# A two-layer decoder step on one core: the eight sample columns move from the second token half to the first, one memory's keys and values move to another stage, and the closing norm is done by tokens

## The chip, the core and the metric

The kernel runs on one core of a Trainium2 chip. The core has a matrix engine (TensorE, in the profile PE, with PEld for its weight loads), a vector engine (VectorE, DVE), a scalar engine for activations (ScalarE, ACT), GpSimdE (POOL) and a queue that issues most transfers (SyncE, SP). The metric is the device time of one execution in microseconds, lower is better.

## The reference

One inference step of a decoder with two layers, model width 1024, in float32. There are two inputs which share all weights: a prompt of 1024 tokens, and 8 samples of one token each with caches of their own.

- Layer 0 has a gated linear recurrence (4 heads, state 128 x 128 each) in parallel with attention into 256 memory tokens (4 heads). The two outputs are joined and multiplied by `w_o`.
- After layer 0 one shared key and value (4 heads x 128) is projected with `w_kv`. Layer 1 has stick-breaking attention over these in parallel with memory attention.
- Each layer ends with a SwiGLU feed-forward of width 2816. Every sub-layer is `h = h + rmsnorm(f(rmsnorm(h, g_in)), g_out)`.
- For the samples the recurrence starts from a given state, the memory's keys and values are read from `cache_mem_k` and `cache_mem_v` (512 KB each for a sample and a layer), and the shared keys and values from a paged cache through `page_table`.
- Memory keys and values of the prompt are `mem_prompt @ w_mem_kv[l]` for each layer `l`, and are outputs too.

```python
q_h, f_h, i_h, g_h, q_m = jnp.split(hn @ w_in, 5, axis=-1)
...
o, S = hgrn2_scan(q, k, v, logf, s0)
o = rmsnorm(o, hg_gain) * silu(g_h)
om = mem_attend(q_m, mem_k, mem_v)
out = jnp.concatenate([o, om], axis=-1) @ w_o
...
h = h + rmsnorm(mix, g[1])
h = h + rmsnorm(swiglu(rmsnorm(h, g[2]), w_gu[l], w_down[l]), g[3])
```

## The kernel before

The prompt is split into two halves of G = 512 tokens, called g = 0 and g = 1. Activations lie transposed: 128 features on the partitions, tokens along the row, eight such tiles for the width of 1024. In the kernel before, the 8 samples are eight more columns (512 to 519) of the second half. NG gives a half's width (512, 520), and since one PSUM bank holds 512 columns, a projection of the wider half is done as two pieces of 260 (PW, NPC).

A projection (`proj`, L256) works on float32 as two rounded parts, high and low: for each of 128 rows of weights it issues three matmuls (high x high, high x low, low x high; L264). Weights come in tiles of 256 KB (`split_w`, DMA L245 on SP), ACT rounds them to the high part (L250) and DVE subtracts for the low part (L251). Five raw and five split tiles rotate. `mmp` holds two PSUM tiles for projections, `smp` three, `nsp` one (`NS()`) that the norms, the memory's transposes and the transposes in `residual` share.

Tiles come from rotating pools. The ones that matter here: `cpool` (`C()`, four buffers of 512 KB, for cache tiles, memory tokens, output rows), `apool` (`A()`, eight, recurrence tensors and layer 1 queries), `rpool` (one buffer, the feed-forward's sum or the prompt's rows), `xpool` (normed inputs, eight for each half). A tile that is asked for waits until the buffer's last reader is done.

Stages are generators, one for each head, block or group. `weave((gen, n), ...)` steps several in the ratio of their numbers, `drain` runs one to its end. That fixes the order in which work is written; a scheduler then makes one fixed list of instructions for each engine, and each engine works through its list in order, waiting where data or a buffer is missing.

The stages in order (L1060 to L1113): the first half's input (`start`, rows are scaled with their norm, transposed at L350), its recurrence inputs (`fq`, `v`), its recurrence (`core`: at seven levels, products L810 on PE and updates L815 to L820 on DVE) woven with the memory's keys and values of both layers; then the second half's input and projections, first half's memory attention (L550 to L581) and output product `o0.mm`, the second half's recurrence (`core`, with the samples' recurrence `hgrn_sample` first, L764 and L767) woven with the first half's feed-forward (`f0.part(0)` to `part(4)`), and so on, with one half's attention beside the other half's feed-forward.

A sample's memory attention (`mem_attn_sample`) has no matmul against the cache: the query is transposed (L597), written to memory and read back onto all partitions (L601, L607), each cache tile is multiplied by it (L608) and reduced (L609) on DVE; after the softmax, each value tile is multiplied (L620), its halves added (L621) and summed over partitions with a matmul (L622). `sb_sample` does the same with tiles gathered through the page table on POOL (L649). `sample_scores` and `sample_pv` hold these loops. In layer 0 they run beside `f0.part(2)` and `part(3)`, in layer 1 likewise.

The end of the kernel: `f1.finish` takes the sum of squares over features with a matmul by ones (L291), Ln and Exp (L292, L293), then for each of eight tiles scales (L382) and adds the residual stream from memory (L388); `store_y` transposes back to rows of tokens (L1042), copies (L1045) and stores (L1047, the samples L1056).

## Time and profile before

| | before |
|---|---|
| runs, us | 2579.38, 2580.38, 2580.97 (median 2580.38) |
| profiled execution, us | 2580.92, of which the span is 2579.2 |
| mean granted clock of TensorE | 0.986 of full speed |
| PE busy | 2538.2 us, 98% |
| PE weight loads, beside it | 2211.0 us, 86% |
| DVE busy | 1563.1 us, 61% |
| ACT busy | 1209.4 us, 47% |
| POOL busy | 47.7 us, 2% |
| read from and written to HBM | 267.57 and 31.93 MB, 116 GB/s over the span |

The profile shows one execution. Busy time counts an engine's own instructions; matmuls overlap in TensorE's pipeline, so that a busy PE can still be a slow one, and its price for one matmul is better read from the distance of two starts. In a row of the order of time stand the start and the length in microseconds, the engine, line, operation, output and inputs, and in square brackets the idle time ahead of it with what ended it. The granted clock of TensorE is in tenths of full speed.

### The profile page before, as it was taken

Reading aid. Unit: us, or ns where it says so; the run is one execution under the profiler, and the core shown is the slowest. Engines: PE = TensorE matmul, PEld = TensorE weight load, DVE = VectorE, ACT = ScalarE, POOL = GpSimd, SP = SyncE. Lnnn points to the kernel's source line nnn. Section 1 sums busy time; section 2 is a strip of 40 time slices with the busy share of each in tenths; the row PEclk is TensorE's granted clock in tenths of the full one; section 3 lists DMA queues with packets and bytes.
Section 4 is the critical chain, followed back from the end, with each engine's and each line's share of the span. In section 5 each row is a group of like instructions: output and inputs, shape, how many; then the busy total and the mean of one; then the engine's idle time right before and its main releaser. Section 6 shows DMA issues by size and latency. Waiting matters only on the chain.

```text
span 2579.2 us, 40377 instructions
## 1 busy us (share of the span) xinstructions
PE 2538.2 (98%) x15603; PEld 2211.0 (86%) x15603; DVE 1563.1 (61%) x2717; ACT 1209.4 (47%) x2274; POOL 47.7 (2%) x59
## 2 busy tenths in 40 slices
PE   8999999999999999999999999999999999999997
PEld 6888887888877888999999989767776788999997
DVE  6666475635765576555544576666678658444445
ACT  6446551245334455555433455566542355443333
POOL 1000000000000000000000000000041000000000
PEclk9999997899999999999999999999999999999998
DMA  6352244132652445322333445322166444323332
GB/s 183 109 168 74 71 153 121 37 87 86 186 166 83 130 149 183 101 85 61 99 91 93 126 148 184 110 87 67 56 186 204 147 152 131 111 84 108 93 91 87
DMA packets 459435, 302.16 MB, mean 117 GB/s; under 512 B 17765, under 2 KB 422834, under 8 KB 459242
## 3 DMA queue, kind: packets, MB, share of 16 engines
q1 hardware_dynamic: 456682, 291.18, 37.6%
q0 software_dynamic: 2560, 8.39, 1.1%
q8 instruction: 123, 2.02, 0.3%
q14 instruction: 70, 0.57, 0.1%
HBM read 267.57 MB, written 31.93 MB: 116 GB/s over the span
## 4 chain that ended last, share of the span: by engine, by line
PE 45%; DVE 2%; issue 1%; DMA 1%; ACT 1%; POOL 0%; DVEq 0%; POOLq 0%; ACTq 0%; SPq 0%
PE mm L264 40%; PE s L980 1%; PE s L992 1%; PE s L965 1%; POOL c L649 0%; PE s L622 0%; PE s L1042 0%; PE ns L291 0%; PE s L581 0%; DMA b<-qd 0%; DVE c L608 0%; DVE sc L609 0%; PE s L550 0%; DVE ws L251 0%; DVE st L302 0%
## 5 line engine op out<-in xcount | busy, mean ns | idle before, releaser
L264 PE MATMUL mm<-x,ws 128*128 128x260 f32 (+1 forms) x10080 | 1672.7, 323 | 10.6 <-DVE ws L251 4.2
L264 PEld LDWEIGHTS mm<-x,ws 128*128 128x128 f32 x10080 | 1448.1, 189 | 174.6 <-issue 26.8
L251 DVE TENSOR_TENSOR ws<-w,ws 128x512 fp32r<-128x512 f32 (+1 forms) x800 | 522.8, 658 | 524.5 <-ACT ws L250 521.9
L250 ACT CAST ws<-w 128x512 fp32r<-128x512 f32 (+1 forms) x800 | 474.3, 593 | 713.3 <-PE mm L264 652.5
L264 PE MATMUL mm<-m,ws 128*128 128x260 f32 (+1 forms) x3168 | 541.1, 325 | 0.7 <-ACT r L399 0.7
L264 PEld LDWEIGHTS mm<-m,ws 128*128 128x128 f32 x3168 | 454.1, 188 | 60.9 <-issue 15.8
L277 ACT ACTIVATE t<-mm 128x520 f32<-128x520 f32 (+1 forms) x104 | 62.5, 601 | 189.7 <-PE mm L264 189.7
L401 DVE TENSOR_TENSOR r<-r,mm 128x520 f32<-128x520 f32 (+1 forms) x128 | 88.4, 691 | 88.9 <-PE mm L264 87.6
L447 DVE TENSOR_TENSOR t<-t,mm 128x512 f32<-128x512 f32 (+1 forms) x88 | 60.9, 692 | 73.3 <-PE mm L264 73.1
L280 DVE SCALAR_TENSOR_TENSOR t<-mm,t 128x520 f32<-128x520 f32 (+1 forms) x104 | 72.2, 694 | 42.4 <-ACT t L279 42.1
L302 DVE TENSOR_TENSOR st<-st,n 128x512 f32<-128x512 f32 (+1 forms) x98 | 67.2, 693 | 7.3 <-ACT n L301 5.6
L281 ACT ACTIVATE t<-t 128x520 f32<-128x520 f32 (+1 forms) x104 | 65.9, 633 | 10.3 <-DVE t L280 10.2
L279 ACT ACTIVATE t<-t 128x520 f32<-128x520 f32 (+1 forms) x104 | 66.0, 635 | 2.7
L278 ACT ACTIVATE t<-t 128x520 f32<-128x520 f32 (+1 forms) x104 | 66.2, 637 | 0.0
L283 DVE TENSOR_TENSOR t<-t,mm 128x512 f32<-128x512 f32 (+1 forms) x88 | 60.4, 686 | 5.5 <-ACT t L281 5.0
L271 ACT CAST m<-t 128x512 fp32r<-128x512 f32 (+1 forms) x88 | 54.9, 624 | 17.1 <-DVE t L447 10.0
L272 DVE TENSOR_TENSOR m<-t,m 128x512 fp32r<-128x512 f32 (+1 forms) x88 | 61.1, 694 | 2.6 <-ACT m L271 0.4
L810 PEld LDWEIGHTS s<-a,a 128*128 128x128 f32 x448 | 57.6, 206 | 1.6 <-PE s L810 0.7
L810 PE MATMUL s<-a,a 128*128 128x64 f32 x448 | 57.9, 286 | 0.5 <-DVE a L817 0.5
L649 POOL DMA_INDIRECT c<-in_cache_sb_k,pidx x16 | 22.7, 1416 | 1882.9 <-DVE r L401 1256.9
L944 DVE SCALAR_TENSOR_TENSOR b<-b,b 128x512 f32<-128x512 f32 (+3 forms) x48 | 26.8, 558 | 30.6 <-ACT b L943 30.1
L561 ACT ACTIVATE b<-s,nmx 128x256 f32<-128x256 f32 x64 | 29.8, 470 | 28.8 <-DVE nmx L555 28.8
(262 smaller groups left out, 1969.9 us busy)
## 6 DMA issues: line engine op xcount, KB each, us to landing
w<-in_w_gu SPq DMA_DIRECT2D x352, 256.0 KB, 2.9
w<-in_w_down SPq DMA_DIRECT2D x160, 256.0 KB, 2.8
w<-in_w_in_a SPq DMA_DIRECT2D x80, 256.0 KB, 3.0
w<-in_w_o SPq DMA_DIRECT2D x64, 256.0 KB, 2.7
w<-in_w_mem_kv SPq DMA_DIRECT2D x32, 256.0 KB, 3.0
c<-in_cache_mem_k SPq DMA_DIRECT2D x16, 512.0 KB, 4.6
c<-in_cache_mem_v SPq DMA_DIRECT2D x16, 512.0 KB, 3.9
w<-in_w_kv SPq DMA_DIRECT2D x32, 256.0 KB, 2.8
```

The lines of the kernel that those rows point to most:

```text
L250: nc.scalar.copy(ws[:, 0, :n, :], raw[:, :n, :])
L251: nc.vector.tensor_sub(ws[:, 1, :n, :], raw[:, :n, :], ws[:, 0, :n, :].bitcast(F32))
L264: nc.tensor.matmul(ps[:, a, : PW[g]], wt, xt[k][:, xi, o : o + PW[g]], start=(k == 0 and wi == 0), stop=(k == nk - 1 and wi == 2),)
L272: nc.vector.tensor_sub(dst[1], src, dst[0].bitcast(F32))
L277: nc.scalar.activation(av, pv(ps, g), AF.Abs)
L278: nc.scalar.activation(av, av, AF.Exp, scale=-1.0)
L279: nc.scalar.activation(av, av, AF.Ln, bias=1.0)
L280: nc.vector.scalar_tensor_tensor(av, pv(ps, g), 0.0, av, op0=ALU.min, op1=ALU.subtract)
L281: nc.scalar.activation(av, av, AF.Exp)
L302: nc.vector.tensor_add(acc[:, :n], acc[:, :n], t[:, :n])
L401: nc.vector.tensor_add(dst, dst, pv(ps, g))
L810: nc.tensor.matmul(plv[:, hh, c, :], K_[:, hh, cs], rhs, start=True, stop=True)
```

## The change

- The 8 sample columns belong to the first half: NG is (520, 512), and all conditions on `g` that concern samples turn round. The samples are read and normed in `start(0)`; `hgrn_sample` is a stage of its own, `a0.sample()`, beside `a0.gate()` and `start(1)`; layer 0's `mem_sample` stands behind `a0.mem()` beside the second half's `fq` and `v`, ahead of `o0.mm`; layer 1's `sb_sample` and `mem_sample` belong to `b0` and stand beside `f1.part(0)` to `part(3)`.
- The second half's V lies in two `cpool` tiles instead of `apool` tiles.
- `mem_load` is done once for each layer, into one tile of `rpool`; layer 1's memory keys and values, and the second half's memory queries, move from the first recurrence to `o0.finish()`, the first output norm.
- The closing norm is by tokens: the last `out_proj` (`last=True`) does not store the residual stream, `token_rows` transposes it to rows, the last feed-forward (`rows=True`) scales its tiles with the gain and transposes the first half of them as soon as four are ready (`first_half`), and `finish_rows` takes the norm per token (a matmul with one column for each 128 tokens), transposes the other four tiles, scales and adds in one step for each half row, and stores.
- Layer 1's second half: its attention stands beside `f0.part(0)` to `part(2)`, and `o1.finish` beside `part(3)`.

```diff
--- before.py
+++ after.py
@@ -38,9 +38,9 @@
     NP = page_table.shape[1]
     SCALE = P ** -0.5
     G = 512
-    NG = [G, G + NB]
-    PW = [G, (G + NB) // 2]
-    NPC = [1, 2]
+    NG = [G + NB, G]
+    PW = [(G + NB) // 2, G]
+    NPC = [2, 1]
     WID = G + NB
     CH = G // P
 
@@ -232,10 +232,10 @@
 
 
     def pv(ps, g):
-        return ps[:, 0, :G] if g == 0 else ps[:, :, : PW[1]]
+        return ps[:, 0, :G] if g else ps[:, :, : PW[0]]
 
     def sv(ap, g):
-        return ap[:, :G] if g == 0 else ap.rearrange("p (a n) -> p a n", a=2)
+        return ap[:, :G] if g else ap.rearrange("p (a n) -> p a n", a=2)
 
     def split_w(W, k0, nk, m0):
         out = []
@@ -329,12 +329,13 @@
             xtok.append(rpool.tile([P, CH, D], F32, tag="r", name="xtok1"))
             for tb in range(CH):
                 nc.sync.dma_start(xtok[g][:, tb, :], x_prompt[0, g * G + tb * P : g * G + (tb + 1) * P, :])
+        if g == 0:
             xs = C().rearrange("p a n -> p (a n)")[:NB]
             nc.sync.dma_start(xs, x_sample.rearrange("b o d -> (b o) d"))
         for tb in range(CH):
             rms_rows(xtok[g][:, tb, :], P)
             yield
-        if g:
+        if g == 0:
             ps = S()
             for k in range(ND):
                 nc.tensor.transpose(ps[:, k * NB : (k + 1) * NB], xs[:, k * P : (k + 1) * P], ident[:NB, :NB])
...
@@ -405,8 +406,8 @@
     class out_proj:
 
 
-        def __init__(self, g, l, store):
-            self.g, self.l, self.store, self.x = g, l, store, []
+        def __init__(self, g, l, store, last=False):
+            self.g, self.l, self.store, self.x, self.last = g, l, store, [], last
 
         def mm(self, xo, m0=0, m1=ND):
             g = self.g
@@ -422,16 +423,32 @@
             g, l = self.g, self.l
             rstd = rstd_from(self.acc, NG[g], 1.0 / D)
             acc = small([P, WID], tag="st", bufs=3)
-            yield from residual(g, self.R, rstd, lambda k: gcol(l, 1, k), True, acc, l == 0)
+            yield from residual(g, self.R, rstd, lambda k: gcol(l, 1, k), not self.last, acc, l == 0)
             r2 = rstd_from(acc, NG[g], 1.0 / D)
             yield
-            yield from normed(g, self.R, r2, lambda k: gcol(l, 2, k), self.x)
+            yield from normed(g, self.R, r2, lambda k: gcol(l, 2, k), self.x, self.last)
+
+    def token_rows(g, R):
+
+        ht = []
+        for c in range(CH):
+            t = apool.tile([P, D], F32, tag="a", name=nm("hT"))
+            for a in range(2):
+                ps = S()
+                for k in range(4):
+                    nc.tensor.transpose(ps[:, k * P : (k + 1) * P], R[4 * a + k][:, c * P : (c + 1) * P], ident)
+                nc.scalar.copy(t[:, a * 512 : (a + 1) * 512], ps)
+            ht.append(t)
+            yield
+        htok.append(ht)
+
+    htok = []
 
     PARTS = [(0, 5), (5, 5), (10, 4), (14, 4), (18, 4)]
 
     class ffn:
-        def __init__(self, g, l, xt):
-            self.g, self.l, self.xt = g, l, xt
+        def __init__(self, g, l, xt, rows=False):
+            self.g, self.l, self.xt, self.rows = g, l, xt, rows
             self.R = self.acc = None
 
         def part(self, pi):
@@ -456,6 +473,12 @@
             for m in range(ND):
                 ps = proj(g, w_down[l], f0, nf, m * P, mids)
                 evac_raw(g, self.R, ps, m, self.acc, pi == 0, last)
+                if last and self.rows:
+                    nc.scalar.activation(
+                        self.R[m][:, :n], self.R[m][:, :n], AF.Copy, scale=gcol(l, 3, m)
+                    )
+                    if m == 3:
+                        self.first_half()
                 if m % 2:
                     yield
 
@@ -467,11 +490,41 @@
                 self.r = rstd_from(acc, NG[self.g], 1.0 / D)
                 yield
 
-
-    memt = []
-
-    def mem_load():
-        memt.extend(xpool.tile([P, 2, 2, NM], F32R, tag="x1", name=nm("memt")) for _ in range(ND // 2))
+        def first_half(self):
+            self.yt = [xpool.tile([P, D], F32, tag="x0", name=nm("yT")) for _ in range(CH)]
+            for c in range(CH):
+                ps = S()
+                for k in range(4):
+                    nc.tensor.transpose(ps[:, k * P : (k + 1) * P], self.R[k][:, c * P : (c + 1) * P], ident)
+                nc.scalar.copy(self.yt[c][:, :512], ps)
+
+        def finish_rows(self):
+
+            ht = htok[0]
+            g, R, acc = self.g, self.R, self.acc
+            ps = NS()
+            for c in range(CH):
+                nc.tensor.matmul(ps[:, c : c + 1], acc[:, c * P : (c + 1) * P], ones[:, 0:1], start=True, stop=True)
+            r = small([P, 8], tag="rr")
+            nc.scalar.activation(r[:, :CH], ps[:, :CH], AF.Ln, scale=1.0 / D, bias=epsb)
+            nc.scalar.activation(r[:, :CH], r[:, :CH], AF.Exp, scale=-0.5)
+            for c in range(CH):
+                o = c * P
+                pt = S()
+                for k in range(4):
+                    nc.tensor.transpose(pt[:, k * P : (k + 1) * P], R[4 + k][:, o : o + P], ident)
+                yt, h, rc = self.yt[c], ht[c], r[:, c : c + 1]
+                nc.vector.scalar_tensor_tensor(yt[:, :512], yt[:, :512], rc, h[:, :512], op0=ALU.mult, op1=ALU.add)
+                nc.vector.scalar_tensor_tensor(yt[:, 512:], pt, rc, h[:, 512:], op0=ALU.mult, op1=ALU.add)
+                t0 = g * G + c * P
+                nc.sync.dma_start(y_prompt[0, t0 : t0 + P, :], yt)
+                yield
+
+
+    memt = [None, None]
+
+    def mem_load(l):
+        memt[l] = rpool.tile([P, ND, 2, NM], F32R, tag="r", name=nm("memt"))
         for tb in range(NM // P):
             xt = C()
             xf = xt.rearrange("p a n -> p (a n)")
@@ -480,12 +533,8 @@
                 ps = NS()
                 for k in range(4):
                     nc.tensor.transpose(ps[:, k * P : (k + 1) * P], xf[:, (a + k) * P : (a + k + 1) * P], ident)
-                for b in range(2):
-                    d = memt[(a + 2 * b) // 2]
-                    split_to(
-                        (d[:, 0, :, tb * P : (tb + 1) * P], d[:, 1, :, tb * P : (tb + 1) * P]),
-                        ps[:, 2 * b * P : (2 * b + 2) * P].rearrange("p (k t) -> p k t", k=2),
-                    )
+                d = memt[l][:, a : a + 4, :, tb * P : (tb + 1) * P]
+                split_to((d[:, :, 0, :], d[:, :, 1, :]), ps.rearrange("p (k t) -> p k t", k=4))
             yield
 
     def mem_keys(l):
...
@@ -698,13 +747,13 @@
             )
 
     def v_proj(g, W, m0, xt, vt, vs):
-        vt.extend((A(), A()))
+        vt.extend((C(), C()) if g else (A(), A()))
         for h in range(H):
             ps = proj(g, W, 0, ND, m0 + h * P, xt)
             t = T()
             nc.scalar.copy(sv(t, g), pv(ps, g))
             to_token(t, vt, h)
-            if g:
+            if g == 0:
                 nc.vector.tensor_copy(vs[:, h, :], t[:, G : G + NB])
             yield
 
@@ -866,7 +915,7 @@
             self.g, self.xt = g, xt
             self.W = w_in_a[0]
             self.F, self.K, self.Q, self.V, self.Qm, self.sg = [], [], [], [], [], []
-            self.vs = small([P, H, NB], tag="vs", bufs=1) if g else None
+            self.vs = None if g else small([P, H, NB], tag="vs", bufs=1)
 
         def fq(self):
             yield from gate_proj(self.g, self.W, self.xt, self.F, self.K)
@@ -875,10 +924,11 @@
         def v(self):
             yield from v_proj(self.g, self.W, 8 * P, self.xt, self.V, self.vs)
 
+        def sample(self):
+            yield from hgrn_sample(self.F, self.K, self.Q, self.vs)
+
         def core(self):
             g = self.g
-            if g:
-                yield from hgrn_sample(self.F, self.K, self.Q, self.vs)
             yield from hgrn_prompt(g, self.F, self.K, self.Q, self.V)
             if g:
                 nc.sync.dma_start(st_prompt[0, 0].rearrange("h k v -> k h v"), carry)
...
@@ -1061,23 +1111,19 @@
     drain(start(0, x0))
     a0 = mixer_a(0, x0)
     drain(a0.fq(), a0.v())
-    weave(
-        (a0.core(), 22),
-        (chain(mem_load(), mem_keys(0), mem_values(0), mem_keys(1), mem_values(1), a0.qm(M)), 22),
-    )
+    weave((a0.core(), 22), (chain(mem_load(0), mem_keys(0), mem_values(0), a0.qm(M)), 14))
     a0.open()
     a1 = mixer_a(1, x1)
-    weave((chain(a0.gate(), a0.merge()), 8), (start(1, x1), 14))
-    weave((a0.mem(), 8), (a1.fq(), 8))
+    weave((a0.sample(), 6), (a0.gate(), 4), (start(1, x1), 12))
+    weave((chain(a0.merge(), a0.mem(), a0.mem_sample()), 32), (chain(a1.fq(), a1.v()), 12))
     o0 = out_proj(0, 0, M)
     drain(o0.mm(a0.xo))
-    weave((o0.finish(), 17), (a1.v(), 4))
+    weave((o0.finish(), 17), (chain(mem_load(1), mem_keys(1), mem_values(1), a1.qm(A)), 14))
     f0 = ffn(0, 0, o0.x)
-    weave((a1.core(), 27), (f0.part(0), 9), (a1.qm(A), 4))
+    weave((a1.core(), 22), (f0.part(0), 9))
     a1.open()
-    weave((chain(a1.gate(), a1.merge()), 8), (f0.part(1), 9))
-    weave((chain(a1.mem_sample(), a1.mem()), 28), (chain(f0.part(2), f0.part(3)), 16))
-    drain(f0.part(4))
+    weave((chain(a1.gate(), a1.merge(), a1.mem()), 16), (chain(f0.part(1), f0.part(2)), 17))
+    drain(f0.part(3), f0.part(4))
     xk0, xb0 = [], []
     o1 = out_proj(1, 0, M)
     drain(o1.mm(a1.xo, 0, 1))
@@ -1089,8 +1135,11 @@
     weave((b0.heads(), 8), (o1.finish(), 17))
     b0.open()
     f1 = ffn(1, 0, o1.x)
-    weave((chain(b0.sb(), b0.mem()), 24), (chain(f1.part(0), f1.part(1)), 18))
-    drain(f1.part(2), f1.part(3), f1.part(4))
+    weave(
+        (chain(b0.sb(), b0.mem(), b0.sb_sample(), b0.mem_sample()), 64),
+        (chain(f1.part(0), f1.part(1), f1.part(2), f1.part(3)), 34),
+    )
+    drain(f1.part(4))
     xk1, xb1 = [], []
     o0 = out_proj(0, 1, M)
     drain(o0.mm(b0.xo, 0, 1))
@@ -1102,15 +1151,14 @@
     weave((b1.heads(), 8), (o0.finish(), 17))
     b1.open()
     f0 = ffn(0, 1, o0.x)
-    weave((chain(b1.sb(), b1.mem()), 40), (chain(f0.part(0), f0.part(1)), 18))
-    weave((chain(b1.sb_sample(), b1.mem_sample()), 40), (chain(f0.part(2), f0.part(3)), 16))
-    o1 = out_proj(1, 1, A)
+    weave((chain(b1.sb(), b1.mem()), 40), (chain(f0.part(0), f0.part(1), f0.part(2)), 26))
+    o1 = out_proj(1, 1, A, True)
     drain(o1.mm(b1.xo))
-    weave((o1.finish(), 17), (f0.part(4), 8))
-    f1 = ffn(1, 1, o1.x)
-    weave((chain(f0.finish(False), store_y(0, f0.R)), 12), (f1.part(0), 9))
-    drain(f1.part(1), f1.part(2), f1.part(3), f1.part(4))
-    drain(f1.finish(False), store_y(1, f1.R))
+    weave((o1.finish(), 17), (f0.part(3), 8))
+    drain(f0.part(4))
+    f1 = ffn(1, 1, o1.x, True)
+    weave((chain(f0.finish(False), store_y(0, f0.R), token_rows(1, o1.R)), 21), (chain(f1.part(0), f1.part(1)), 18))
+    drain(f1.part(2), f1.part(3), f1.part(4), f1.finish_rows())
 
 
 _INS = [
```

16 lines of the change are left out of this document (8 added, 8 removed).

## The prediction

> **What bounds the kernel now.** I read the head of the page first (busy shares and the clock), then the busy time by stretch, then the order of time at the places where TensorE (PE) falls short. The median of the three runs is 2580.38 us; the profiled execution took 2580.92 us, 0.02% above it, and the sum below is made against 2580.92.
>
> ```profile
> span 2579.2 us, 40377 instructions
> PE 2538.2 (98%) x15603; PEld 2211.0 (86%) x15603; DVE 1563.1 (61%) x2717; ACT 1209.4 (47%) x2274; POOL 47.7 (2%) x59
> PEclk9999997899999999999999999999999999999998
> ```
>
> PE is busy for 98%, DVE for 61%: the span is the length of PE's stream, and a change gains only where PE idles or runs slowly. The granted clock dips around the seventh slice and at the end. By stretch (columns: span, then PE, PEld, DVE, ACT and POOL busy, clock, DMA share, GB/s):
>
> ```profile
> 380.00:400.00 20.00, 20.00 (x105) 14.62 (x104) 15.54 (x22) 5.71 (x10) 0.00 (x0) 0.92 0.57 158
> 400.00:420.00 20.00, 20.00 (x61) 14.22 (x59) 5.19 (x7) 0.62 (x1) 0.00 (x0) 0.50 0.53 144
> 420.00:440.00 20.00, 19.96 (x103) 16.96 (x104) 13.73 (x28) 5.78 (x12) 0.00 (x0) 0.90 0.35 120
> 460.00:480.00 20.00, 19.50 (x138) 19.26 (x137) 18.55 (x65) 0.62 (x1) 0.00 (x0) 0.80 0.10 27
> 480.00:500.00 20.00, 17.80 (x79) 14.96 (x79) 6.06 (x17) 6.75 (x12) 0.00 (x0) 0.78 0.05 14
> 660.00:720.00 60.00, 60.00 (x266) 48.87 (x265) 47.26 (x63) 26.22 (x45) 0.00 (x0) 1.00 0.72 215
> 1900.00:1920.00 20.00, 15.77 (x58) 11.96 (x57) 20.00 (x23) 6.01 (x10) 15.14 (x9) 0.83 0.77 238
> 1980.00:2000.00 20.00, 16.31 (x65) 12.53 (x64) 19.91 (x25) 7.05 (x12) 0.00 (x0) 0.94 0.74 235
> ```
>
> These stretches are, in order: the samples' recurrence (hgrn_sample, at 0.92, 0.50 and 0.90), the end of the second half's recurrence, layer 0's sample memory attention, which costs PE nothing (60.00 of 60), and layer 1's two sample score phases, in which DVE is full (20.00) and PE waits. Prices on PE come from starts that follow each other:
>
> ```profile
> 428.40 5.73 PE L264 MATMUL mm<-x,ws 128*128 128x512 f32 x24
> 433.97 1.90 PE L810 MATMUL s<-a,a 128*128 128x64 f32 x16
> 441.24 5.47 PE L810 MATMUL s<-a,a 128*128 128x64 f32 x48
> 446.79 5.78 PE L264 MATMUL mm<-x,ws 128*128 128x512 f32 x24
> 454.79 5.99 PE L264 MATMUL mm<-x,ws 128*128 128x260 f32 x48
> 460.62 8.46 PE L810 MATMUL s<-a,a 128*128 128x64 f32 x74
> L381 PE MATMUL ns<-ident,ht 128*128 128x128 f32 x64 | 9.8, 275 | 0.0
> ```
>
> A 512-column matmul takes (433.97 - 428.40)/24 = 0.232 us, two of 260 take 2 x (460.62 - 454.79)/48 = 0.243, a 64-column one (446.79 - 441.24)/48 = 0.116. A 128-column transpose lies between 0.116 and 9.8/64 = 0.153; I take 0.12.
>
> **The change part by part.**
>
> *Sample columns to the first half, as such.* The count of projections in the form with 2 x 260 columns equals that with 512 in both programs: 0. What counts is where the sample work lands.
>
> *The tail (closing norm by tokens).*
>
> ```profile
> 2544.83 7.50 PE L264 MATMUL mm<-m,ws 128*128 128x260 f32 x61
> 2553.83 0.70 DVE L302 TENSOR_TENSOR st<-st,n 128x520 f32<-128x520 f32 x1 [0.76 <-ACT n L301]
> 2556.91 0.27 ACT L292 ACTIVATE st<-ns,epsb 128x8 f32<-128x8 f32 x1 [0.48 <-PE ns L291]
> 2557.88 1.43 DVE L382 SCALAR_TENSOR_TENSOR r<-r,par,st 128x520 f32<-128x520 f32 x2 [3.35 <-ACT st L293]
> 2571.09 3.12 SPq L1047 DMA_DIRECT2D out_y_prompt<-c  x4
> 2575.51 0.30 SPq L1056 DMA_DIRECT2D out_y_sample<-c  x1
> ```
>
> Now the last projection ends at 2544.83 + 7.50 = 2552.3, and 26.9 us follow: sum of squares, norm, eight pairs of DVE steps, transposes, copies, stores. Afterwards: the same 2.2 to the sum of squares (2552.3 to 2554.5), eight matmuls of one column at 0.116 with the 0.48 that ACT waited ahead of L292, 1.4, Ln and Exp on four columns 0.6 (two of 0.27 and a handover), eight steps on DVE at 1.43/2 = 0.72, 5.7, and the last store, 4 (the sample store of before ends 3.7 after its issue at 2575.51; this one is 512 KB). Together 14: a gain of 13 (10 to 14). The transposes lie before or beside this.
>
> *More work on PE outside the tail.* 16 transposes of the second mem_load, 32 of token_rows, 16 of first_half, and the samples' 8 of store_y, out of the tail now: 72 x 0.12 = 8.6; I take 8. Nothing covers it, since PE is the bound. The 8 ACT scalings, the ACT copies and the smaller number of splits lie on engines with room: 0; without that cover 16 such steps, at the 0.72 of L382, would be 11.5. The eight stores and four loads of hs less on SP: 0, since PE waits for none of them.
>
> *Layer 1's samples.*
>
> ```profile
> L608 DVE TENSOR_TENSOR c<-c,b 128x1024 f32<-128x1024 f32 x24 | 29.0, 1223 | 5.3 <-DMA b<-qd 5.3
> L609 DVE TENSOR_REDUCE sc<-c 128x8 f32<-128x1024 f32 x24 | 28.9, 1215 | 0.0
> L621 DVE TENSOR_TENSOR c<-c 128x512 f32<-128x512 f32 x24 | 16.0, 687 | 0.0
> ```
>
> They leave the second half (lines sb_sample, mem_sample) and stand beside four parts of the first half's feed-forward instead of two. Lost now: idle 4.2 + 3.7, and by the clock 20 x 0.17 + 20 x 0.06 = 4.6, together 12.5. In the new order one score phase stands beside some 150 projections of 0.232, that is 35 us; DVE has 8 x (1.22 + 1.22) = 19.5 us of scores and, for each 48 matmuls (11 us), some nine steps of 512 columns at 0.69, 6.2, so 19 or 20 in 35: 39 against 35, though the steps around a phase have room; I take 1 lost in each phase. Gain 10.5 (6 to 12).
>
> *The second half's recurrence* spreads over f0.part(0) without the sample recurrence ahead of it; no level run on PE exceeds 24 program matmuls, with 5.7 us or more of projections between. Lost now in 460 to 500: idle 0.5 + 2.2, clock 4.0 + 4.4, 11.1. Left about 3, where groups follow without cover. Gain 8 (5 to 10).
>
> *The samples' recurrence* beside a0.gate and start(1): lost now by the clock 10 + 2, and 1.6 in the stretch before, 13.6. The new order still has one dense run of such matmuls (about 3.7 us), with 5 us of projections behind it. I take 5 lost; gain 8.6 (0 to 13). The row shows half clock at PE busy 20.00. The Trainium skill (TensorE: Matmul & The Clock Gate, Part 1: The HAM clock gate) has the clock halve after an idle window of about 3.4 us; by that alone nothing would be lost here and this term would be 0, the sum 8.6 higher. The row speaks against it: the clock fell without an idle PE, among matmuls with few columns or rows.
>
> *start(0).*
>
> ```profile
> 12.22 0.76 DVE L325 TENSOR_SCALAR xtok<-xtok,rr 128x1024 f32<-128x1024 f32 x1 [0.35 <-ACT rr L324]
> 12.41 0.68 POOL L197 TENSOR_SCALAR pidx<-ptb 128x16 int32<-128x16 int32 x1 [2.29 <-DMA ptb<-in_page_table]
> 15.48 0.79 PE L264 MATMUL mm<-x,ws 128*128 128x512 f32 x1 [1.33 <-ACT x L353]
> ```
>
> The load of the samples is issued behind the page table's, which landed at 12.41. PE's transposes of it stand ahead of all others and DVE's copy (xsraw) ahead of three of the four row scalings, the last of which now starts at 12.22. These three are queued behind that wait, and the first projection behind them: 2 to 2.5 later, and the small evacuations of 8 columns add to each x: +4 (2 to 6).
>
> *a0's memory attention for the samples, directly ahead of o0.mm.* This is the largest cost.
>
> ```profile
> 1890.92 0.27 PE L597 MATMUL s<-ident,ss 128*8 128x128 f32 x1
> 1899.03 1.23 DVE L608 TENSOR_TENSOR c<-c,b 128x1024 f32<-128x1024 f32 x1 [0.77 <-DMA b<-qd]
> 1918.02 2.35 DVE L609 TENSOR_REDUCE sc<-c 128x8 f32<-128x1024 f32 x2
> 672.45 0.67 DVE L599 COPY b<-s 8x512 f32<-8x512 f32 x1
> 678.25 1.23 DVE L608 TENSOR_TENSOR c<-c,b 128x1024 f32<-128x1024 f32 x1 [2.42 <-DMA b<-qd]
> 710.30 1.22 DVE L609 TENSOR_REDUCE sc<-c 128x8 f32<-128x1024 f32 x1
> 729.70 1.23 DVE L620 TENSOR_TENSOR c<-c,ss 128x1024 f32<-128x1024 f32 x1
> 754.40 1.02 PE L622 MATMUL s<-c,sel 128*8 128x512 f32 x2
> c<-in_cache_mem_v SPq DMA_DIRECT2D x16, 512.0 KB, 3.9
> ```
>
> Scores: from the query's transposes to the last reduction 1890.92 to 1920.4, 29.5 us. The second half's own in layer 0 took 672.45 to 711.5, 39, and its values 729.70 to 755.4, 25.7, with four buffers. Here 8 us until the query is back, 8 x 2.44 = 19.5 on DVE, a few steps between: 28 to 30. PE's order has 77 projections of 512 columns in that time, 77 x 0.232 = 17.9, and 0.6 more: 10 idle. Values: the second half's V now holds two of the four buffers, so a load waits until PE has used the tile two before it, in order with its projections: 3.9 load, 1.22 + 0.69 on DVE, 0.5 on PE, about 6.7 for two tiles, 27 for eight, 7 until the first stands, 3 at the end: 36 to 37. PE has 55 projections of 512 and 50 of 260 columns there, 12.8 + 6.1, transposes 1.9 and the sums 3.7: 24.5, so 11 to 12 idle. Before o0.mm's k of 4 and above nothing else may run. Together 21 (10 to 34): the low end if the loads land under the projections, the high end with scores as slow as 672 to 711 and a half clock afterwards.
>
> *mem_load, keys and values of layer 1 at o0.finish:* more cover for it than a1.v gave; but one small PSUM buffer serves residual, loader and norm in turn, and DMAs queue on SP ahead of ht's: +1 (0 to 5). *a0.core* with fewer such projections: 16 level matmuls (3.7) and 12 of mem_values (2.8) against about 6 on DVE for each level: +2 (0 to 5). *b1.mem then o1.mm* without samples between: +1 (0 to 4).
>
> Sum: gains 13 + 10.5 + 8 + 8.6 = 40; costs 8 + 4 + 21 + 1 + 2 + 1 = 37; net -3: 2578.
>
> **Rivals.** About 0.2% (5.2 us) is what a measurement of this kernel tells from no change: 2575.2 and 2585.5.
> (a) Cover suffices ahead of o0.mm: the stall is 5, net -19, 2562. For it: 60.00 of 60 in 660 to 720 for the same work; against it: 18 us of projections under a chain of 28.
> (b) Slower: that stall alone. With the scores at the pace of 672 to 711 (39 us) PE idles 20, and with the values 12 and two slow restarts 2: 34, net +10, 2591. It decides from a stall of about 29 on. For it: PE waits for DVE and DMA there in order; against: DVE's list there has fewer steps between.
> (c) The clock stays halved through the samples' recurrence as before: the gain of 8.6 is gone, net +6, 2587; the part doesn't do its work. For it: the same matmuls, still dense.
>
> **How the numbers follow.** Forecast (stall 15 to 28, 2572 to 2585): 0.42, of which 0.14 lies below 2575.2, 0.25 within and 0.03 above. (a) 0.26, (b) 0.20, (c) 0.12. Faster 0.40, same 0.25, slower 0.35. Range: from halfway between (a) and its best terms, 2557, to (b) with the start at its worst, 2598; the forecast's own is 2572 to 2585.
>
> **What would show it.** Right: from the last projection to the end 14 us; 20.00 on PE in layer 1's sample stages; two stretches ahead of o0.mm with PE idle about 10 each while DVE runs products and waits for cache_mem_v; first projection at 18 us. Wrong: no idle there (then 2562), or a clock of 0.5 for over 15 us in the samples' recurrence, or a new PE wait in b0's feed-forward or in o0.finish.

## The result and the profile after

The changed kernel takes 2591.99 us (median of six runs, 2587.60 to 2594.28) against 2579.88 us for the kernel before (six runs, 2579.19 to 2581.54). The ratio is 1.0044, with a 95% interval of 1.0031 to 1.0057: slower by 0.44%. The profiled execution took 2591.94 us, 11.0 more than that of before, at a mean granted clock of 0.989 against 0.986.

```profile
span 2590.2 us, 40466 instructions
PE 2529.7 (98%) x15657; PEld 2210.1 (85%) x15657; DVE 1560.7 (60%) x2706; ACT 1220.3 (47%) x2289; POOL 39.8 (2%) x59
PEclk9999989999999999999999999999999999999999
```

PE is busy for 8.5 us less than before in a span that is 11 us longer. The half clock in the seventh slice and at the end has mostly gone, and PE idles instead. By stretch (the columns are those of the prediction):

```profile
200.00:220.00 20.00, 20.00 (x105) 15.77 (x105) 11.08 (x16) 7.11 (x16) 0.00 (x0) 0.74 0.42 120
220.00:240.00 20.00, 20.00 (x151) 17.92 (x149) 14.91 (x26) 10.53 (x21) 0.00 (x0) 1.00 0.63 199
300.00:320.00 20.00, 9.78 (x36) 7.64 (x35) 17.18 (x18) 4.57 (x8) 0.00 (x0) 0.74 0.70 219
320.00:340.00 20.00, 17.87 (x84) 13.27 (x83) 13.74 (x21) 7.38 (x16) 0.00 (x0) 1.00 0.56 162
340.00:360.00 20.00, 15.23 (x76) 8.99 (x74) 11.30 (x13) 3.31 (x7) 0.00 (x0) 0.94 0.68 204
360.00:380.00 20.00, 16.92 (x103) 14.09 (x102) 5.95 (x11) 4.58 (x11) 0.00 (x0) 0.72 0.27 81
400.00:420.00 20.00, 17.92 (x146) 17.02 (x144) 12.82 (x25) 7.35 (x13) 0.00 (x0) 0.98 0.54 185
420.00:440.00 20.00, 17.09 (x113) 15.04 (x112) 16.81 (x35) 8.56 (x16) 0.00 (x0) 0.77 0.34 110
460.00:580.00 120.00, 120.00 (x949) 116.88 (x948) 71.71 (x167) 42.62 (x78) 0.00 (x0) 1.00 0.31 90
1280.00:1300.00 20.00, 17.09 (x65) 12.61 (x64) 18.46 (x26) 4.30 (x9) 11.68 (x11) 0.91 0.66 183
1260.00:1420.00 160.00, 153.19 (x643) 115.57 (x642) 120.86 (x175) 56.56 (x107) 29.09 (x28) 0.99 0.64 194
1900.00:1920.00 20.00, 19.89 (x138) 17.74 (x137) 13.67 (x30) 11.06 (x23) 0.00 (x0) 1.00 0.35 101
1980.00:2000.00 20.00, 19.86 (x139) 18.15 (x138) 11.13 (x25) 8.84 (x23) 0.00 (x0) 1.00 0.22 65
```

The first two are the samples' recurrence, 300 to 380 is layer 0's sample memory attention ahead of `o0.mm`, 400 to 440 the first output norm, 460 to 580 the second half's recurrence, 1280 the first half's sample scores in layer 1, and 1260 to 1420 the whole stretch with the two score phases of the samples there; at 1900 and 1980, where the samples used to stand, PE is full.

PE's order of time through the sample memory attention shows where PE stands still. Line numbers differ from before: L657 and L658 are the score products and reductions, L669 and L670 the value products, L671 their sums, L283 a projection's last evacuation step.

```profile
295.00 7.88 PE L264 MATMUL mm<-x,ws 128*128 128x512 f32 x33
313.10 11.22 PE L264 MATMUL mm<-x,ws 128*128 128x512 f32 x41 [10.22 <-DVE a L283]
337.31 1.02 PE L671 MATMUL s<-c,sel 128*8 128x512 f32 x2 [2.13 <-DVE c L670]
359.16 1.87 PE L671 MATMUL s<-c,sel 128*8 128x512 f32 x2 [3.74 <-DVE c L670]
363.34 1.87 PE L671 MATMUL s<-c,sel 128*8 128x512 f32 x2 [2.31 <-DVE c L670]
```

On DVE, the same stretch:

```profile
303.31 2.36 DVE L657 TENSOR_TENSOR c<-c,b 128x1024 f32<-128x1024 f32 x2 [2.82 <-DMA b<-qd]
322.68 1.21 DVE L658 TENSOR_REDUCE sc<-c 128x8 f32<-128x1024 f32 x1
334.63 1.22 DVE L669 TENSOR_TENSOR c<-c,ss 128x1024 f32<-128x1024 f32 x1 [3.52 <-DMA c<-in_cache_mem_v]
350.05 1.23 DVE L669 TENSOR_TENSOR c<-c,ss 128x1024 f32<-128x1024 f32 x1 [3.03 <-DMA c<-in_cache_mem_v]
361.34 1.22 DVE L669 TENSOR_TENSOR c<-c,ss 128x1024 f32<-128x1024 f32 x1 [2.23 <-PE s L671]
```

For 10.22 us PE cannot start a projection: both PSUM tiles wait for L283, and L283 stands in DVE's list among the score products that began at 303.31. Then DVE waits for value tiles (3.52, 3.03) and once more at the end (2.23). The row puts that last wait down to PE's sum at L671; but the load of its tile, issued at 356.12, landed only at 360.9, so it is at least as likely what ended the wait. Together PE idles 10.22 + 2.13 + 4.77 + 3.08 = 20.2 us between 300 and 380. At the first output norm:

```profile
417.19 0.66 PE L535 MATMUL ns<-ident,c 128*128 128x128 f32 x4 [0.65 <-DVE m L385]
419.29 1.11 PE L535 MATMUL ns<-ident,c 128*128 128x128 f32 x4 [1.44 <-DVE memt L272]
421.80 1.12 PE L382 MATMUL ns<-ident,ht 128*128 128x128 f32 x4 [1.40 <-DVE memt L272]
423.70 1.11 PE L535 MATMUL ns<-ident,c 128*128 128x128 f32 x4 [0.78 <-DVE m L385]
```

The transposes of `mem_load` (L535) and of the residual (L382) share one PSUM buffer and wait for each other's readers on DVE, and nothing else is in PE's order until the keys' projections (L548) begin at 425.49, 8.3 us after the loader's first transpose. The start, and the tail:

```profile
12.60 1.02 PE L341 MATMUL s<-ident,c 8*128 8x8 f32 x8 [6.79 <-DMA c<-in_x_sample]
17.91 1.10 PE L264 MATMUL mm<-x,ws 128*128 128x260 f32 x2 [0.78 <-ACT x L354]
2567.40 9.75 PE L264 MATMUL mm<-m,ws 128*128 128x512 f32 x41
2579.32 1.05 PE L507 MATMUL ns<-ones,st 128*128 128x1 f32 x8 [1.18 <-DVE st L302]
2580.94 0.75 DVE L517 SCALAR_TENSOR_TENSOR yT<-yT,rr,hT 128x512 f32<-128x512 f32 x1 [1.68 <-ACT rr L510]
2585.57 0.75 DVE L518 SCALAR_TENSOR_TENSOR yT<-s,rr,hT 128x512 f32<-128x512 f32 x1
```

The first projection starts at 17.91 instead of 15.48, held by the sample load. The last one ends at 2567.40 + 9.75 = 2577.15, 13.0 us ahead of the span's end, instead of 26.9.

The terms, between the two profiled executions (plus is time lost). The losses of the clock and of the waits are read as in the prediction: PE's idle time, and half of the time that PE is busy at half clock. The tail and the start are differences of length. The row on `a0.core` is that stretch's length less its matmuls at the prediction's prices, good to about 1 us, and the row on the work on PE is a count, not a measurement.

| term | predicted | measured |
|---|---|---|
| tail | -13 | -13.8 |
| layer 1's samples, with b1.mem to o1.mm | -9.5 | -4 (12.1 less in the second half, 8.1 more in the first) |
| second half's recurrence | -8 | -11 |
| samples' recurrence | -8.6 | -8.4 (13.6 before, 5.2 after) |
| more work on PE | +8 | +8.6 (72 transposes at the predicted 0.12) |
| start(0) | +4 | +2.4 |
| a0's sample memory attention | +21 | +26 (20.2 idle, the rest at half clock) |
| layer 1's mem_load, keys and values at the first norm | +1 | +8.5 (5.0 idle, 3.6 at half clock, 0.1 before) |
| a0.core | +2 | +3 (PE idles 0.7) |
| sum | -3 | +11, of 11.0 |

### The profile page after: what moved, and what is told of

Its sections match the earlier page's. It is cut to its first block, busy times and chain, and to the rows that moved or that the text cites. A ratio compares the mean times of both kernels' runs of the same rounds, so it can differ in the third digit from the quotient of the medians.

```text
span 2590.2 us, 40466 instructions
## 1 busy us (share of the span) xinstructions
PE 2529.7 (98%) x15657; PEld 2210.1 (85%) x15657; DVE 1560.7 (60%) x2706; ACT 1220.3 (47%) x2289; POOL 39.8 (2%) x59
## 5 line engine op out<-in xcount | busy, mean ns | idle before, releaser
L264 PE MATMUL mm<-x,ws 128*128 128x260 f32 (+1 forms) x10080 | 1667.0, 323 | 13.7 <-DVE a L283 10.2
L264 PEld LDWEIGHTS mm<-m,ws 128*128 128x128 f32 x3168 | 460.7, 189 | 65.9 <-issue 8.3
L277 ACT ACTIVATE t<-mm 128x512 f32<-128x512 f32 (+1 forms) x104 | 62.5, 601 | 181.8 <-PE mm L264 181.6
L402 DVE TENSOR_TENSOR r<-r,mm 128x512 f32<-128x512 f32 (+1 forms) x128 | 88.2, 690 | 97.5 <-PE mm L264 96.2
L464 DVE TENSOR_TENSOR t<-t,mm 128x520 f32<-128x520 f32 (+1 forms) x88 | 60.8, 691 | 76.4 <-PE mm L264 76.0
L280 DVE SCALAR_TENSOR_TENSOR t<-mm,t 128x512 f32<-128x512 f32 (+1 forms) x104 | 72.1, 693 | 39.9 <-ACT t L279 39.9
L281 ACT ACTIVATE t<-t 128x512 f32<-128x512 f32 (+1 forms) x104 | 65.8, 633 | 13.9 <-DVE t L280 13.8
L302 DVE TENSOR_TENSOR st<-st,n 128x520 f32<-128x520 f32 (+1 forms) x98 | 67.1, 691 | 6.9 <-ACT n L301 4.8
L279 ACT ACTIVATE t<-t 128x512 f32<-128x512 f32 (+1 forms) x104 | 66.1, 636 | 2.8
L283 DVE TENSOR_TENSOR t<-t,mm 128x520 f32<-128x520 f32 (+1 forms) x88 | 60.3, 686 | 11.2 <-ACT t L281 10.9
L278 ACT ACTIVATE t<-t 128x512 f32<-128x512 f32 (+1 forms) x104 | 66.3, 637 | 0.0
L272 DVE TENSOR_TENSOR m<-t,m 128x520 fp32r<-128x520 f32 (+1 forms) x88 | 61.0, 694 | 3.3 <-ACT m L271 0.9
L271 ACT CAST m<-t 128x520 fp32r<-128x520 f32 (+1 forms) x88 | 54.9, 623 | 17.2 <-DVE t L464 10.1
L1042 PE MATMUL s<-b,a 128*128 128x512 f32 (+3 forms) x96 | 41.2, 511 | 0.5 <-DVE b L997 0.3
```

Of the source, the lines that this page charges most:

```text
L264: nc.tensor.matmul(ps[:, a, : PW[g]], wt, xt[k][:, xi, o : o + PW[g]], start=(k == 0 and wi == 0), stop=(k == nk - 1 and wi == 2),)
L277: nc.scalar.activation(av, pv(ps, g), AF.Abs)
L278: nc.scalar.activation(av, av, AF.Exp, scale=-1.0)
L279: nc.scalar.activation(av, av, AF.Ln, bias=1.0)
L280: nc.vector.scalar_tensor_tensor(av, pv(ps, g), 0.0, av, op0=ALU.min, op1=ALU.subtract)
L281: nc.scalar.activation(av, av, AF.Exp)
```

## Experiments

The theory (1): the loss is layer 0's sample memory attention, a chain over DVE and transfers that the projections beside it don't cover, and behind it the norm. Rivals: (2) the norm's loss, or more, is `mem_load` sharing the norms' one PSUM buffer; (3) what remains is the clock in the samples' recurrence, decided by how dense the sample matmuls stand. The kernel before, measured beside each set, took 2579.5, 2579.5, 2580.4 and 2580.7 us; "after" is the changed kernel's 2592.0. Experiments start from the changed kernel.

**Without layer 0's sample memory attention.** Zeros are written in its place.

```diff
-            yield from mem_attn_sample(0, self.Qm, self.xo)
+            z = small([P, NB], tag="ss")
+            nc.vector.memset(z, 0.0)
+            for h in range(H):
+                d = self.xo[H + h]
+                split_to((d[:, 0, G : G + NB], d[:, 1, G : G + NB]), z)
+            yield
```

> Leaves out the samples' memory attention of layer 0 (zeros take the place of its result). The changed kernel's profile has PE idle 10.2 us once and 10 us in pieces between the samples' query transposes (292.9 us) and the return of o0.mm (367.4), and a half clock around them. Theory 1, that this stall ahead of o0.mm is the largest cost: the stall with its clock (29) and the step's own work on PE (16 matmuls at 0.43 and a few transposes, 8) go, 2592 - 37 = 2555 (2550 to 2562). Rival, that what is lost lies in the first output norm and in layer 1 and the stall only takes the place of other waits: 2575 or more.

Measured: 2558.1 us (2555.3 to 2562.1), ratio to before 0.9913 [0.9897, 0.993], 33.9 less than after. The attention's own sums on PE are eight pairs of L671, about 1 us each; what remains of the 33.9, some 25, agrees with the 26 of the stall. The norm still loses, here from 380 to 400:

```profile
380.00:400.00 20.00, 15.03 (x98) 12.79 (x96) 17.61 (x38) 7.05 (x13) 0.00 (x0) 0.83 0.19 66
```

PE is idle for 5 us there, at a granted clock of 0.83. So theory 1 holds for the stall, and the norm's loss isn't a consequence of it.

**V in `apool` again, queries beside the recurrence.** This gives all four cache buffers back to the value tiles.

```diff
-        vt.extend((C(), C()) if g else (A(), A()))
+        vt.extend((A(), A()))
...
-    weave((o0.finish(), 17), (chain(mem_load(1), mem_keys(1), mem_values(1), a1.qm(A)), 14))
+    weave((o0.finish(), 17), (chain(mem_load(1), mem_keys(1), mem_values(1)), 10))
...
-    weave((a1.core(), 22), (f0.part(0), 9))
+    weave((a1.core(), 22), (f0.part(0), 9), (a1.qm(A), 4))
```

> The second half's V goes back to two apool tiles, so that the sample's value tiles have four buffers instead of two; for want of apool tiles the second half's memory queries go back beside its recurrence. Theory 1a, that the value phase waits for buffers: it falls from 36 us to about 25, PE idles 10 less, 2582 (2578 to 2586). Rival, that the loads' own time and the fixed order of the lists set it: 2591 to 2593. If the first output norm needs the queries as cover, it loses up to 5 more there, 2587.

Measured: 2584.8 us (2580.0 to 2592.1), 1.0018 [1.0007, 1.003], 7 less than after.

```profile
300.00:320.00 20.00, 10.88 (x42) 8.57 (x41) 15.61 (x17) 6.28 (x11) 0.00 (x0) 0.77 0.83 263
340.00:360.00 20.00, 19.40 (x106) 13.02 (x105) 11.25 (x18) 5.66 (x15) 0.00 (x0) 1.00 0.58 188
460.00:580.00 120.00, 116.37 (x885) 110.79 (x885) 63.08 (x153) 40.15 (x73) 0.00 (x0) 1.00 0.26 78
```

The wait for value tiles was the two missing buffers: 340 to 360 goes from 15.23 to 19.40, and over the whole value phase PE idles 0.6 us instead of 10.0. The scores' stall stays (10.88), and 3.6 us of idle come in 460 to 580, in the second half's recurrence, where the queries now stand.

**More projections beside the attention.** The second half's memory queries, 96 matmuls of projections, move from the norm to the attention.

```diff
-    weave((chain(a0.merge(), a0.mem(), a0.mem_sample()), 32), (chain(a1.fq(), a1.v()), 12))
+    weave((chain(a0.merge(), a0.mem(), a0.mem_sample()), 32), (chain(a1.fq(), a1.v(), a1.qm(A)), 16))
...
-    weave((o0.finish(), 17), (chain(mem_load(1), mem_keys(1), mem_values(1), a1.qm(A)), 14))
+    weave((o0.finish(), 17), (chain(mem_load(1), mem_keys(1), mem_values(1)), 10))
```

> The second half's memory queries (96 matmuls of 0.2265, 22 us) move from the first output norm to beside the samples' memory attention. Theory 1: the missing cover of 20 us is mostly filled, 2592 - 16 = 2576 (2572 to 2582), with up to 4 lost in the output norm. Rival, that the value tiles with two buffers take as long whatever stands beside and in order with them: 2586 to 2592.

Measured: 2572.5 us (2569.9 to 2583.2), 0.9979 [0.9966, 0.9992]: 19.5 less than after, and faster than before.

```profile
300.00:320.00 20.00, 18.22 (x84) 14.45 (x83) 17.98 (x21) 9.18 (x18) 0.00 (x0) 1.00 0.71 222
320.00:340.00 20.00, 18.03 (x79) 12.55 (x78) 14.21 (x20) 6.42 (x14) 0.00 (x0) 1.00 0.69 197
340.00:360.00 20.00, 19.85 (x71) 11.18 (x69) 14.15 (x17) 4.67 (x9) 0.00 (x0) 1.00 0.77 223
420.00:440.00 20.00, 17.07 (x113) 15.30 (x114) 17.57 (x38) 8.25 (x15) 0.00 (x0) 0.76 0.32 106
```

PE's idle time from 300 to 360 falls from 17.1 us to 3.9, and the clock stays at 1.00. From the query's transposes to the last sum the attention takes 67 us, where after has 71: it is hardly shorter, it is covered. The norm's row is that of after.

**`mem_load` in the projections' small buffers.**

```diff
-                ps = NS()
+                ps = S()
```

> mem_load transposes into the three smp buffers instead of the one that the norm and the residual's transposes use. In the changed kernel 11 us are lost on PE from o0.mm to the recurrence, where the prediction had 1 more than the 4 of before. Theory 2, that the single PSUM buffer in turn does this: 5 less, 2587 (2584 to 2589). Rival, that the norm's start (sum of squares, half clock, subtractions on DVE) does it: 2591 to 2593.

Measured: 2591.7 us (2586.4 to 2596.8), 1.005 [1.0034, 1.0066]: no gain in time. Its profiled execution (2591.70 us) did lose less at the norm:

```profile
220.00:240.00 20.00, 20.00 (x102) 16.43 (x102) 8.94 (x13) 5.21 (x11) 0.00 (x0) 0.66 0.55 173
400.00:420.00 20.00, 19.09 (x161) 18.85 (x161) 6.85 (x11) 8.78 (x16) 0.00 (x0) 1.00 0.52 158
420.00:440.00 20.00, 20.00 (x160) 18.88 (x161) 18.88 (x38) 11.81 (x23) 0.00 (x0) 1.00 0.61 201
440.00:460.00 20.00, 19.20 (x87) 14.70 (x87) 18.57 (x32) 12.52 (x23) 0.00 (x0) 1.00 0.77 239
```

From 400 to 460 PE idles 1.7 us at full clock, where after loses 8.6 at the norm, and the keys' projections begin 3.2 us after the loader's first transpose instead of 8.3. So in this execution the one buffer accounts for 7 of the norm's 8.6 us. The same execution lost more by the clock elsewhere: 5 us in the samples' recurrence (0.66 against 1.00 in 220 to 240), ahead of the norm, and 4 at the attention. In time rival (2) is therefore not shown; at its place the trace bears it out.

**Only `mem_load` ahead of the norm**, beside `o0.mm`.

```diff
-    drain(o0.mm(a0.xo))
-    weave((o0.finish(), 17), (chain(mem_load(1), mem_keys(1), mem_values(1), a1.qm(A)), 14))
+    weave((o0.mm(a0.xo), 8), (mem_load(1), 2))
+    weave((o0.finish(), 17), (chain(mem_keys(1), mem_values(1), a1.qm(A)), 12))
```

> The changed kernel with the only difference that layer 1's mem_load stands beside o0.mm. If the loader at the head of the norm costs 6 there, 2586 (2583 to 2589). Its two tiles of cpool are asked for as soon as the samples' last value tiles are free, so a longer value phase could take a part of it back; the rival, no gain, 2591 to 2593.

Measured: 2587.5 us (2583.5 to 2589.9), 1.003 [1.0019, 1.0042], 4.5 less than after.

```profile
400.00:420.00 20.00, 20.00 (x162) 19.21 (x161) 7.28 (x11) 8.63 (x17) 0.00 (x0) 1.00 0.61 201
420.00:440.00 20.00, 20.00 (x150) 18.35 (x149) 19.23 (x40) 10.88 (x22) 0.00 (x0) 1.00 0.64 210
```

The norm's loss is gone: the loader is done, so the keys' projections can run from the norm's first step on, and the queries last to its end. In the runs' time that is worth 4.5 us, with an interval that still overlaps that of after. The edit also takes the loader off the norm's buffer while the norm runs, so it doesn't tell the buffer from the order.

**Both at once.** To the queries at the attention comes the early `mem_load`.

```diff
-    drain(o0.mm(a0.xo))
-    weave((o0.finish(), 17), (chain(mem_load(1), mem_keys(1), mem_values(1)), 10))
+    weave((o0.mm(a0.xo), 8), (mem_load(1), 2))
+    weave((o0.finish(), 17), (chain(mem_keys(1), mem_values(1)), 8))
```

> As the version with the queries as cover (2572.5), and layer 1's mem_load (its transposes and splits) beside o0.mm instead of at the head of the output norm, so that the norm starts beside projections that can run at once. Theory 2b: the 10 us that every version so far loses from the end of o0.mm into the norm come from having only the loader's transposes, each behind a step on DVE, as cover: 6 less, 2566 (2563 to 2569). Rival, that the norm's own chain (two sums of squares, residual, DVE) costs them whatever is beside it: 2571 to 2574.

Measured: 2572.1 us (2570.8 to 2582.4), 0.9971 [0.9961, 0.9981]: the 2572.5 of the queries alone, a miss. PE's order of time and the stretch that holds it:

```profile
460.24 1.22 PE L575 MATMUL mm<-ws,memt 128*128 128x512 f32 x2 [4.01 <-DVE ws L572]
440.00:460.00 20.00, 15.26 (x78) 11.78 (x76) 18.01 (x31) 11.31 (x21) 0.00 (x0) 1.00 0.52 158
```

The loss has moved to the norm's end, where only `mem_values` (L575) is left beside it and waits for its split weights on DVE (L572), which the norm keeps busy (18.01 of 20). The norm wants cover at both ends, and the queries can't be in two places.

**Queries divided.** Two of the queries' four steps go to the attention, two stay behind keys and values.

```diff
+    def take(gen, n):
+        for _ in range(n):
+            yield next(gen)
...
+    q1 = a1.qm(A)
-    weave((chain(a0.merge(), a0.mem(), a0.mem_sample()), 32), (chain(a1.fq(), a1.v()), 12))
+    weave((chain(a0.merge(), a0.mem(), a0.mem_sample()), 32), (chain(a1.fq(), a1.v(), take(q1, 2)), 14))
-    drain(o0.mm(a0.xo))
-    weave((o0.finish(), 17), (chain(mem_load(1), mem_keys(1), mem_values(1), a1.qm(A)), 14))
+    weave((o0.mm(a0.xo), 8), (mem_load(1), 2))
+    weave((o0.finish(), 17), (chain(mem_keys(1), mem_values(1), q1), 10))
```

> From the changed kernel: two of the second half's four memory query heads (11 us of projections) stand beside the samples' memory attention, two at the end of the first output norm, and layer 1's mem_load beside o0.mm. The profiles so far: the norm loses 10 wherever nothing but the loader's transposes (at its head) or mem_values (at its end) is left to run, and 2 where queries stand at its end. If so, the stall ahead of o0.mm falls by 11 to 13 and the norm's 10 by 6 to 8: 2592 - 18 = 2574, or 2568 if the clock restarts go too (2566 to 2576). Rival, that cover taken from one place is missed at the other: 2580 or more.

Measured: 2571.4 us (2568.7 to 2578.1), 0.9969 [0.9959, 0.9979]: the lowest median of all, 20.6 less than after and 9 less than before, but not told apart from the two versions above.

```profile
320.00:340.00 20.00, 15.08 (x60) 10.65 (x61) 16.61 (x23) 4.66 (x10) 0.00 (x0) 0.91 0.68 197
420.00:440.00 20.00, 19.51 (x130) 17.14 (x129) 19.74 (x39) 10.75 (x20) 0.00 (x0) 1.00 0.69 225
```

The norm is covered (19.51 against 17.07); 4.9 us of idle return at the attention.

**Samples before the prompt's memory attention.**

```diff
-    weave((chain(a0.merge(), a0.mem(), a0.mem_sample()), 32), (chain(a1.fq(), a1.v()), 12))
+    weave((chain(a0.merge(), a0.mem_sample(), a0.mem()), 32), (chain(a1.fq(), a1.v()), 12))
```

> The changed kernel with the order of two parts turned: the samples' memory attention ahead of the prompt's (a0.mem), so that o0.mm waits for the short one. By PE's order 93 projections of 0.2265 stand in the score phase (21 us, before 18) and some 80 in the value phase, which has all four buffers as V comes later. If what counts is the length of the chain against the projections beside it: 8 idle in the scores, 5 to 8 in the values instead of 20, 2592 - 8 = 2584 (2579 to 2588). Rival, that the wait counts because it stands last ahead of o0.mm: nearly all of the 29 goes, 2565.

Measured: 2595.6 us (2585.2 to 2599.2), 1.005 [1.0033, 1.0068]: no gain, a miss.

```profile
287.63 1.22 PE L264 MATMUL mm<-x,ws 128*128 128x512 f32 x2 [8.87 <-DVE a L283]
```

The scores still hold DVE's list, and with it L283, for 8.87 us: the prompt's attention behind them can't pass in the engine's order. The profiled execution took 2599.2, near the slow end of the five. In it the attention lost 20.5 us instead of 27, about what was expected, but the samples' recurrence, ahead of the edit, lost 15.4 by the clock instead of 5.1. What the order is worth can't be read from these five runs. With the same order on top of the divided queries:

```diff
-    weave((chain(a0.merge(), a0.mem(), a0.mem_sample()), 32), (chain(a1.fq(), a1.v(), take(q1, 2)), 14))
+    weave((chain(a0.merge(), a0.mem_sample(), a0.mem()), 32), (chain(a1.fq(), a1.v(), take(q1, 2)), 14))
```

> Both: the split queries with the loader beside o0.mm, and the samples' memory attention first. If the effects add: 4 to 8 less than the split alone, 2566 (2562 to 2572). If the order only moves the same idle time: as the split alone.

Measured: 2572.6 us (2571.6 to 2579.0), 0.9974 [0.9963, 0.9985], the same as without it.

**The tail of before** in the changed kernel.

```diff
-    o1 = out_proj(1, 1, A, True)
+    o1 = out_proj(1, 1, A)
-    f1 = ffn(1, 1, o1.x, True)
+    f1 = ffn(1, 1, o1.x)
...
-    weave((chain(f0.finish(False), store_y(0, f0.R), token_rows(1, o1.R)), 21), (chain(f1.part(0), f1.part(1)), 18))
-    drain(f1.part(2), f1.part(3), f1.part(4), f1.finish_rows())
+    weave((chain(f0.finish(False), store_y(0, f0.R)), 13), (chain(f1.part(0), f1.part(1)), 18))
+    drain(f1.part(2), f1.part(3), f1.part(4), f1.finish(False), store_y(1, f1.R))
```

> The changed kernel with the closing norm of before (features first, store_y at the end). The time from the last projection to the end is 26.9 us before and 13.4 in the changed kernel; token_rows and first_half put 48 transposes of 0.11, 5.3 us, into PE's stream. If both count in full: 2592 + 13.5 - 5 = 2600 (2598 to 2603). Rival, that the transposes ran in time that PE had idle anyway: 2605.

Measured: 2601.7 us (2598.0 to 2606.4), 1.0087 [1.0067, 1.0106]. The closing norm by tokens is worth 9.7 us, its transposes paid.

**All of `f1` beside layer 1's samples**, on top of the queries at the attention.

```diff
-        (chain(f1.part(0), f1.part(1), f1.part(2), f1.part(3)), 34),
+        (chain(f1.part(0), f1.part(1), f1.part(2), f1.part(3), f1.part(4)), 42),
...
-    drain(f1.part(4))
```

> As the version with the queries as cover (2572.5), and the first half's attention and samples of layer 1 stand beside all five parts of f1 instead of four. In the changed kernel 6 us more than before are lost between the two kv projections, where the samples' scores fill DVE. If cover per step decides, 3 to 5 less: 2568 (2566 to 2571). Rival, that DVE's order within each score phase decides, whatever the ratio: 2571 to 2574.

Measured: 2576.5 us (2574.4 to 2579.0), 0.9987 [0.9978, 0.9997], 4 above the version that it starts from: a miss. Layer 1's samples lost 7.6 us in the profiled execution, where the version that it starts from lost 8.3: next to no gain. The 4 us don't lie there. This execution lost 10.2 us by the clock in the samples' recurrence, ahead of the edit and with the same order on PE, the other 5.1; and the mean granted clock is 0.991 to 0.993 in its ten runs, but 0.993 to 0.995 in seven of the ten runs of the other. That the waits in layer 1 are set by DVE's order and not by what PE has beside them is argued, not shown.

**Sample matmuls further apart**, for theory 3: the first half's memory queries move beside the samples' recurrence.

```diff
-    weave((a0.core(), 22), (chain(mem_load(0), mem_keys(0), mem_values(0), a0.qm(M)), 14))
+    weave((a0.core(), 22), (chain(mem_load(0), mem_keys(0), mem_values(0)), 10))
...
-    weave((a0.sample(), 6), (a0.gate(), 4), (start(1, x1), 12))
+    weave((a0.sample(), 6), (chain(a0.gate(), a0.qm(M)), 8), (start(1, x1), 12))
```

> The changed kernel with the first half's memory queries (22 us of projections) moved from beside its recurrence to beside the samples' recurrence, so that no run of eight-row and one-column matmuls lasts over 2 us; before them stand 4 to 9 projections, after them 24 to 30. Every profile so far shows half clock from 200 to 203 us on, for 7 to 10 us, and in most a second time from 218 to 224 for 14 to 24. Theory 3, that the dense run decides: no half clock between 190 and 260 us, 5 to 12 less there, and some 4 lost in the recurrence that has less beside it: 2586 (2582 to 2591). Rival, that the share of such matmuls over a longer time, or something else at that place, decides: half clock there again, and 2592 to 2598.

Measured: 2596.4 us (2589.8 to 2600.6), 1.0054 [1.0033, 1.0075].

```profile
180.00:200.00 20.00, 20.00 (x97) 17.69 (x96) 13.98 (x18) 8.73 (x23) 0.00 (x0) 0.66 0.58 158
```

In PE's order of time the projections that stand between two groups:

```profile
184.89 5.57 PE L264 MATMUL mm<-x,ws 128*128 128x260 f32 x26
```

The clock falls here too, three times for 6.8 us between 183 and 224, with 26 projections between groups (0.21 us each in this row, where 0.12 is the full pace). Theory 3 falls in this form.

## Why the prediction was wrong

The time of 2592.0 lies inside the range, 14 above the forecast of 2578 and on the other side of before; the likeliest sign was wrong. Rival (b), 2591, came nearest, but by luck: the place is the one that it named, its stall was 34, and 26 were found; the first norm and layer 1 made up the rest. The steps that failed are the price of the clock around the stall, the first norm, and layer 1's samples.

- **The stall ahead of `o0.mm`** ("Together 21"): right in place, mechanism and idle time, but 26 and not 21. Predicted were 10 at the scores and 11 to 12 at the values, found 10.22 and 9.98. At the values that is luck in part, as two errors met: the phase took 41.3 us (from 322.68 + 1.21 on DVE to 363.34 + 1.87 on PE) and not 36 to 37, and PE's sums in it, priced at 3.7, take 8, eight pairs of L671 at 1.02. (The 25.7 us that the prediction reads for the values of before are misread too: two more pairs of sums end at 766.47 + 1.88, 38.7 after the start. The term was not built on it.) Not in the sum was the slow clock around each wait (0.74 from 300 to 320, 0.72 from 360 to 380; L671 takes 1.87 there instead of 1.02), about 6; only rival (b) had it, as two slow restarts of 2 together. The experiment with more projections shows it from the other side: without the idle time the clock stays at 1.00. The half clock here begins at 306.4, 3.5 us after PE fell idle at 302.9, and at 357.6, 2.2 us after PE fell idle at 355.4, and lasts 10.2 and 13.7 us. The Trainium skill (TensorE: Matmul & The Clock Gate, Part 1: The HAM clock gate) has the clock halve after an idle window of about 3.4 us and come back after a busy one; the first place agrees with that, the second fell sooner, and the lengths are three and four such windows. At the norm the clock halved at 419.0 with no idle piece over 1.44 us.
- **The first norm** ("+1 (0 to 5)"): 8.5 measured. The prediction named what was at work, one small PSUM buffer that serves residual, loader and norm in turn, and put it at 1 on the grounds that there is more cover than `a1.v` gave. But the keys' projections can't begin before `mem_load` is all but done, so at the norm's head there was no cover for 8.3 us. Moving the loader alone took the loss away, which is worth 4.5 us in the runs; giving the loader other buffers took 7 us of it away in one execution.
- **The tail** is right to 0.8 us, and the start came out 1.6 better. **The work on PE** isn't tested by the table, whose row is the prediction's own count and price. The experiment's 9.7 is the tail's 13.8 less the 48 transposes that `token_rows` and `first_half` put ahead of it; at the predicted 0.12 each that would be 8.0.
- **The second half's recurrence** gained 11 instead of 8: nothing is left of its loss (120.00 of 120 at 1.00).
- **Layer 1's samples** ("I take 1 lost in each phase"): gone from the second half as predicted, but beside the first half's feed-forward 8.3 us are lost in two phases (6.8 idle from 1260 to 1420, and 1.5 at half clock), about 4 in each. The prediction's own count had 39 us on DVE against 35 of projections, 4 over, and was then set at 1. No experiment takes this loss away, so what sets it stays open.
- **The samples' recurrence** came out at 8.4, as forecast, in the two profiled executions. That is luck: with the same order on PE the stage lost up to 15.4 in other changed versions, as the last section shows, so the term can't be given one value. Rival (c) is true of some executions. Rival (a), full cover, is refuted by 20.2 us of idle.

The sum went wrong by 14: about 5 from the stall, 7.5 from the norm, 5.5 from layer 1 and 1 from `a0.core`, less some 5 where terms came out better.

## What to carry to other kernels

A long chain over DVE and transfers costs nothing beside a long run of matmuls, and 26 us beside a short one; before moving such a chain, count the matmuls beside it in microseconds against the chain, and count a slow restart behind each wait that remains. Cover has to be ready when the wait begins: projections behind a load, or behind an evacuation in the same engine's list, are none. Here moving half of one projection stage from the norm to the attention, and the loader ahead of the norm, turned a loss of 0.44% into a gain of 0.31% (0.21 to 0.41) over the kernel before.
